# Linear attention on one core: K, V and Q in 4 KB runs over four heads, groups in order, one PSUM pool, the copy of the transposed Q shared by two engines, halved last store

## The chip, the cores and the metric

One core of one Trainium2 chip runs the kernel. The metric is the device time of an execution in microseconds, as a median of several runs; lower is better. A ratio is the mean time of one kernel's fast runs over the mean time of the fast runs of the kernel before in the same rounds, so it is not quite the ratio of the medians quoted beside it. "Span" is the time from the first to the last instruction in one profiled execution; the device time is one to two microseconds longer.

In lines of the profile PE is TensorE, PEld its weight loads, DVE VectorE, ACT ScalarE, POOL GpSimd and SP SyncE. PSUM is the memory that TensorE writes its results to; here it is handed out in eight banks. A row tile is a part of TensorE's rows that one matmul uses. The granted clock is the share of full speed that TensorE was given; "low clock" means 0.5.

## The reference

```python
Q, K, V: float32 (8, 12, 512, 64), normal
Q_feat = np.maximum(0, Q) + 1
K_feat = np.maximum(0, K) + 1
KV = np.einsum('bhkd,bhkv->bhdv', K_feat, V)
K_sum = np.sum(K_feat, axis=2)
numerator = np.einsum('bhqd,bhdv->bhqv', Q_feat, KV)
denominator = np.einsum('bhqd,bhd->bhq', Q_feat, K_sum)
return (numerator / (denominator[:, :, :, None] + 1e-10)).astype(np.float32)
```

## The kernel before

The 96 heads are worked in 12 groups of eight heads. A group loads 1 MiB each of K, V and Q from HBM (cast to bf16 on the way) and stores 1 MiB. Its stages: VectorE makes the features of K and Q; ScalarE copies V into a layout with a column of ones; TensorE accumulates K-features by V (with the sums in the extra column), transposes Q's features, and multiplies the two; VectorE divides. The schedule is a software pipeline: features of one group, first matmul of the group before, output of the one before that.

```python
k_dram = view(K, C)        # C = 8: runs of 8 x 64 x 4 B = 2 KB; Q has view(Q, 2 * C)
...
psum_qt = tile_pool(name="psum_qt", bufs=2)    # 1 bank each
psum_kva = tile_pool(name="psum_kva", bufs=1)  # 2 banks
psum_out = tile_pool(name="psum_out", bufs=2)  # 2 banks each
...
def kv_and_transpose(g):                        # first matmul: two row tiles of 64
    ...
    for half in range(2):
        qt_ps = psum_qt.tile([P, C, P], BF16)   # one PSUM tile for each half
        for c in range(C):
            nc.tensor.transpose(qt_ps[:, c, :], qf[:, half * C + c, :, :], identity)
        nc.scalar.copy(out=qt[:, :, :, half], in_=qt_ps)
...
for it in range(NG + 2):
    if it < NG: features(it)
    if 1 <= it < NG + 1: kv_and_transpose(it - 1)
    if it >= 2: output(it - 2)
    if it + IN_BUFS < NG: load(it + IN_BUFS)
    if it - LAG >= 0: store(it - LAG)
```

Of the kernel before, what the change touches and what calls it, by code (L numbers as in the profile page):

```python
# [8 lines left out]
FP32 = mybir.dt.float32  # L9
BF16 = mybir.dt.bfloat16  # L10
ALU = mybir.AluOpType

BANK = 512
VP = 130
IN_BUFS = 4
OUT_BUFS = 6
LAG = 3


@with_exitstack  # L20
def kernel(
    ctx: ExitStack,
    tc: tile.TileContext,
    Q: bass.AP,
    K: bass.AP,
    V: bass.AP,
    out: bass.AP,
):






    nc = tc.nc

    B, H, S, D = Q.shape
    P = 128
    C = 8
    C2 = 2 * C  # L40
    NPAIR = B * H * S // (P * C)
    NP = 4
    NG = NPAIR // NP
    D1 = D + 1
    W = 2 * D + 1

    def view(t, c):
        return t.flatten_outer_dims().rearrange("(n p c) d -> p n c d", p=P, c=c)

    q_dram = view(Q, C2)  # L50
    k_dram = view(K, C)
    v_dram = view(V, C)
    o_dram = view(out, C)

    const = ctx.enter_context(tc.tile_pool(name="const", bufs=1))
    head_pool = ctx.enter_context(tc.tile_pool(name="head_pool", bufs=1))
    in_pool = ctx.enter_context(tc.tile_pool(name="in_pool", bufs=IN_BUFS))
    feat_pool = ctx.enter_context(tc.tile_pool(name="feat", bufs=2))
    mid_pool = ctx.enter_context(tc.tile_pool(name="mid", bufs=3))
    out_pool = ctx.enter_context(tc.tile_pool(name="out_pool", bufs=OUT_BUFS))  # L60
    recip_pool = ctx.enter_context(tc.tile_pool(name="recip", bufs=4))
    psum_qt = ctx.enter_context(tc.tile_pool(name="psum_qt", bufs=2, space=bass.MemoryType.PSUM))
    psum_kva = ctx.enter_context(tc.tile_pool(name="psum_kva", bufs=1, space=bass.MemoryType.PSUM))
    psum_out = ctx.enter_context(tc.tile_pool(name="psum_out", bufs=2, space=bass.MemoryType.PSUM))

    identity = const.tile([P, P], BF16, name="identity")
    NV = 2
    v_aug = [const.tile([P, 2, C, VP], BF16, name=f"v_aug{i}") for i in range(NV)]

    raw = {}  # L70
    feat = {}
    mid = {}
    outs = {}

    def load(g):
        first = g == 0
        k_raw = (head_pool if first else in_pool).tile(
            [P, NP, C, D], FP32 if first else BF16, name="k_raw"
        )
        v_raw = in_pool.tile([P, NP, C, D], BF16, name="v_raw")  # L80
        q_raw = in_pool.tile([P, 2, C2, D], BF16, name="q_raw")
        (nc.sync if first else nc.gpsimd).dma_start(  # L82
            out=k_raw, in_=k_dram[:, g * NP : g * NP + NP]
        )
        nc.gpsimd.dma_start(out=v_raw, in_=v_dram[:, g * NP : g * NP + NP])  # L85
        nc.gpsimd.dma_start(out=q_raw, in_=q_dram[:, g * 2 : g * 2 + 2])  # L86
        raw[g] = (k_raw, v_raw, q_raw)

    def store(g):
        nc.gpsimd.dma_start(out=o_dram[:, g * NP : g * NP + NP], in_=outs.pop(g))  # L90

    def feature(dst, src):
        nc.vector.tensor_scalar(  # L93
            out=dst, in0=src, scalar1=1.0, scalar2=1.0, op0=ALU.add, op1=ALU.max
        )

    def features(g):
        k_raw, v_raw, q_raw = raw.pop(g)
        kf = feat_pool.tile([P, 2, C, 2, D], BF16, name="kf")
        qf = feat_pool.tile([P, C2, 2, D], BF16, name="qf")  # L100
        va = v_aug[g % NV]
        for h in range(2):
            feature(kf[:, h].rearrange("p c n d -> p n c d"), k_raw[:, h:NP:2])
            nc.scalar.copy(  # L104
                out=va[:, h].rearrange("p c (n x) -> p n c x", n=2)[:, :, :, 0:D],
                in_=v_raw[:, h:NP:2],
            )
        feature(qf.rearrange("p c n d -> p n c d"), q_raw)
        feat[g] = (kf, qf)

    def kv_and_transpose(g):
        kf, qf = feat.pop(g)
        va = v_aug[g % NV]
        kva_ps = psum_kva.tile([P, 2, BANK], FP32, name="kva_ps")
        for h in range(2):
            for c in range(C):
                for j in range(2):
                    nc.tensor.matmul(  # L118
                        kva_ps[:, j, h * W : h * W + W],
                        lhsT=kf[64 * j : 64 * j + 64, h, c, :, :],  # L120
                        rhs=va[64 * j : 64 * j + 64, h, c, 0:W],
                        start=(c == 0),
                        stop=(c == C - 1),
                    )
        kva = mid_pool.tile([P, 2, 2, D1 + 1], BF16, name="kva")
        for n in range(2):
            nc.scalar.copy(  # L127
                out=kva[64 * n : 64 * n + 64, :, :, 0:D1],
                in_=kva_ps[64 * n : 64 * n + 64, :, 0 : 2 * W].rearrange(
                    "p j (h x) -> p j h x", h=2  # L130
                )[:, :, :, D * n : D * n + D1],
            )

        qt = mid_pool.tile([P, C, P, 2], BF16, name="qt")
        for half in range(2):
            qt_ps = psum_qt.tile([P, C, P], BF16, name="qt_ps")
            for c in range(C):
                nc.tensor.transpose(qt_ps[:, c, :], qf[:, half * C + c, :, :], identity)  # L138
            nc.scalar.copy(out=qt[:, :, :, half], in_=qt_ps)  # L139
        mid[g] = (kva, qt)  # L140

    def output(g):
        kva, qt = mid.pop(g)
        o_sb = out_pool.tile([P, NP, C, D], FP32, name="o_sb")
        for h in range(2):
            ops = [psum_out.tile([P, 2, BANK], FP32, tag="o_ps", name="o_ps") for _ in range(2)]
            for c in range(C):
                off = (c % 4) * D1
                for n in range(2):
                    for j in range(2):  # L150
                        b = 2 * h + j
                        nc.tensor.matmul(  # L152
                            ops[n][64 * j : 64 * j + 64, c // 4, off : off + D1],
                            lhsT=qt[64 * n : 64 * n + 64, c, 32 * b : 32 * b + 32, :],
                            rhs=kva[64 * n : 64 * n + 64, j, h, 0:D1],
                            start=True,
                            stop=True,
                        )
            for n in range(2):
                cells = ops[n][:, :, 0 : 4 * D1].rearrange("p b (r x) -> p b r x", x=D1)  # L160
                den = cells[:, :, :, 0:1] if n else cells[:, :, :, D:D1]
                num = cells[:, :, :, 1:D1] if n else cells[:, :, :, 0:D]
                recip = recip_pool.tile([P, 2, 4, 1], FP32, name="recip")
                nc.vector.reciprocal(out=recip, in_=den)  # L164
                nc.vector.tensor_tensor(  # L165
                    out=o_sb[:, 2 * n + h].rearrange("p (b r) d -> p b r d", b=2),
                    in0=num,
                    in1=recip.to_broadcast([P, 2, 4, D]),
                    op=ALU.mult,
                )  # L170
        outs[g] = o_sb

    with tc.manual_schedule():
        for g in range(IN_BUFS):
            load(g)
            if g == 0:
                make_identity(nc, identity)
                for t in v_aug:
                    nc.gpsimd.memset(t[:, :, :, D : D + 1], 1.0)  # L179
        for it in range(NG + 2):  # L180
            if it < NG:
                features(it)
            if 1 <= it < NG + 1:
                kv_and_transpose(it - 1)
            if it >= 2:
                output(it - 2)
            if it + IN_BUFS < NG:
                load(it + IN_BUFS)
            s = it - LAG
            if s >= 0:  # L190
                store(s)
        for s in range(NG + 2 - LAG, NG):
            store(s)


# [28 lines left out]
```

## Time and profile before

| | before |
|---|---|
| device time, median | 131.0 us (130.81 to 132.17, three runs; 131.12 with the fourth) |
| span of the profiled run | 129.8 us |
| moved to and from HBM | 37.75 MB read, 12.58 MB written |
| busy: PE, DVE, ACT | 46%, 44%, 48% of the span |

Read this profile from the transfers: compute engines are half idle, and the chain of work that ended last, followed back from the end, is 72% transfers. The lines that carry this are in the prediction. In a group's line the figures are busy time, mean ns of one, and the idle time of the engine just before them.

```profile
DMA 72%; issue 19%; POOL 4%; POOLq 1%
...
L139 ACT COPY qt<-qt_ps 128x1024 bf16<-128x1024 bf16 x24 | 29.5, 1298 | 0.4
```

Both halves of qt are copied by ScalarE, 1.3 us each, and ScalarE hardly waits for them.

### The profile page before, as it was taken

To read this page: it belongs to the slowest core of one execution; us is meant where nothing else is said; L and a number is where in the kernel's file an instruction comes from. 1 tells how busy PE (TensorE), PEld (TensorE's weight loads), DVE (VectorE), ACT (ScalarE), POOL (GpSimd) and SP (SyncE) were. 2 spreads that over 40 slices of the span, in tenths; PEclk is the share of its full clock that TensorE was granted. 3 is DMA by queue.
4 is the path that set the end of the run, shared out by engine and by line. 5 is a ranking of instruction groups with operands and counts; after the bars stand their busy time and mean duration, and the time that the engine had idled before them with its cause. 6 is when DMAs were issued, how large, how long until landed. Compare 5 with 4: busy or idle time off the path is not lost.

```text
span 129.8 us, 3048 instructions
## 1 busy us (share of the span) xinstructions
PE 59.0 (46%) x1344; PEld 50.5 (39%) x1344; DVE 57.7 (44%) x132; ACT 62.6 (48%) x73; POOL 36.1 (28%) x55
## 2 busy tenths in 40 slices
PE   0008309208758292864939119409606802933200
PEld 0007209107647191753828009308505701922100
DVE  0222212057374775727577077066227407567700
ACT  3023086590966939296690590391095096270000
POOL 6972224222332242224224222422231200202020
PEclk9999965555686959555595865875785685595555
DMA  2999999999999999999999999999999999999853
GB/s 93 321 204 195 210 194 204 210 206 211 205 209 208 209 207 206 210 207 207 277 302 207 253 331 205 231 350 191 218 347 223 212 357 418 420 417 360 341 218 121
DMA packets 19213, 32.17 MB, mean 248 GB/s; under 512 B 768, under 2 KB 12544, under 8 KB 19200
## 3 DMA queue, kind: packets, MB, share of 16 engines
q0 software_dynamic: 18672, 30.94, 106.3%
q1 hardware_dynamic: 528, 1.05, 2.1%
q8 instruction: 10, 0.16, 0.5%
q14 instruction: 3, 0.02, 0.0%
HBM read 37.75 MB, written 12.58 MB: 388 GB/s over the span
## 4 chain that ended last, share of the span: by engine, by line
DMA 72%; issue 19%; POOL 4%; POOLq 1%
DMA out_dram<-o_sb 31%; DMA k_raw<-in_K_dram 16%; DMA q_raw<-in_Q_dram 15%; DMA v_raw<-in_V_dram 9%; POOL out_dram L90 2%; POOLq L219 1%; POOL q_raw L86 1%; POOL k_raw L82 0%; POOL v_raw L85 0%; POOL identity masks.py:199 0%; POOL identity masks.py:197 0%; POOL v_aug L179 0%; POOLq L90 0%; POOLq L86 0%; POOLq L208 0%
## 5 line engine op out<-in xcount | busy, mean ns | idle before, releaser
L104 ACT COPY v_aug<-v_raw 128x1024 bf16<-128x1024 bf16 x24 | 24.1, 1056 | 48.6 <-DMA v_raw<-in_V_dram 48.6
L152 PE MATMUL o_ps<-kva,qt 64*64 64x65 bf16 x768 | 17.3, 229 | 46.9 <-DVE o_sb L165 45.8
L165 DVE TENSOR_TENSOR o_sb<-o_ps,recip 128x512 f32<-128x512 f32 x48 | 33.2, 691 | 1.6
L152 PEld LDWEIGHTS <-qt 64*64 64x64 bf16 x768 | 12.7, 137 | 52.0 <-DVE o_sb L165 48.9
L139 ACT COPY qt<-qt_ps 128x1024 bf16<-128x1024 bf16 x24 | 29.5, 1298 | 0.4
L118 PE MATMUL kva_ps<-v_aug,kf 64*128 64x129 bf16 x384 | 22.3, 302 | 15.4 <-ACT v_aug L104 10.1
L93 DVE TENSOR_SCALAR qf<-q_raw 128x2048 bf16<-128x2048 bf16 x12 | 8.3, 694 | 42.2 <-DMA q_raw<-in_Q_dram 42.2
L118 PEld LDWEIGHTS <-kf 64*128 64x128 bf16 x384 | 19.1, 137 | 16.2 <-issue 15.6
L138 PE MATMUL qt_ps<-identity,qf 128*128 128x128 bf16 x192 | 21.7, 303 | 0.1
L90 POOL DMA_DIRECT2D out_dram<-o_sb x12 | 9.3, 774 | 38.2 <-DVE o_sb L165 19.6
L138 PEld LDWEIGHTS <-qf 128*128 128x128 bf16 x192 | 18.8, 142 | 2.6 <-issue 2.2
L93 DVE TENSOR_SCALAR kf<-k_raw 128x1024 bf16<-128x1024 bf16 (+1 forms) x24 | 9.8, 450 | 11.2 <-DMA k_raw<-in_K_dram 11.1
L164 DVE RECIPROCAL recip<-o_ps 128x8 f32<-128x8 f32 x48 | 9.6, 201 | 10.5 <-PE o_ps L152 10.5
L85 POOL DMA_DIRECT2D v_raw<-in_V_dram x12 | 9.1, 759 | 17.0 <-ACT kva L127 5.4
L82 POOL DMA_DIRECT2D k_raw<-in_K_dram x11 | 8.6, 786 | 16.7 <-DVE kf L93 6.6
L86 POOL DMA_DIRECT2D q_raw<-in_Q_dram x12 | 8.4, 702 | 15.9 <-DMA k_raw<-in_K_dram 9.0
L127 ACT CAST kva<-kva_ps 64x260 bf16<-64x260 f32 x24 | 8.8, 367 | 3.5 <-PE kva_ps L118 3.4
L104 ACT ACT_TABLE_LOAD x1 | 1.3, 1283 | 0.7 <-PEq L208 0.7
masks.py:199 POOL TENSOR_SCALAR_AFFINE_SELECT identity<-identity 128x128 bf16<-128x128 bf16 x1 | 0.3, 287 | 0.1
masks.py:197 POOL MEMSET identity<- 128x128 bf16 x1 | 0.2, 244 | 0.0
L179 POOL MEMSET v_aug<- 128x16 bf16 x2 | 0.2, 175 | 0.0
L208 POOL MEMSET const-float32-0.0<- 128x1 f32 x1 | 0.1, 99 | 0.2 <-issue 0.2
(3 smaller groups left out, 0.3 us busy)
## 6 DMA issues: line engine op xcount, KB each, us to landing
out_dram<-o_sb POOLq DMA_DIRECT2D x12, 1024.0 KB, 20.0
v_raw<-in_V_dram POOLq DMA_DIRECT2D x12, 512.0 KB, 19.7
q_raw<-in_Q_dram POOLq DMA_DIRECT2D x12, 512.0 KB, 19.8
k_raw<-in_K_dram POOLq DMA_DIRECT2D x11, 512.0 KB, 19.7
k_raw<-in_K_dram SPq DMA_DIRECT2D x1, 1024.0 KB, 5.0
```

The lines of the kernel that those rows point to most:

```text
L85: nc.gpsimd.dma_start(out=v_raw, in_=v_dram[:, g * NP : g * NP + NP])
L86: nc.gpsimd.dma_start(out=q_raw, in_=q_dram[:, g * 2 : g * 2 + 2])
L90: nc.gpsimd.dma_start(out=o_dram[:, g * NP : g * NP + NP], in_=outs.pop(g))
L93: nc.vector.tensor_scalar(out=dst, in0=src, scalar1=1.0, scalar2=1.0, op0=ALU.add, op1=ALU.max)
L104: nc.scalar.copy(out=va[:, h].rearrange("p c (n x) -> p n c x", n=2)[:, :, :, 0:D], in_=v_raw[:, h:NP:2],)
L118: nc.tensor.matmul(kva_ps[:, j, h * W : h * W + W], lhsT=kf[64 * j : 64 * j + 64, h, c, :, :], rhs=va[64 * j : 64 * j + 64, h, c, 0:W], st ...
L127: nc.scalar.copy(out=kva[64 * n : 64 * n + 64, :, :, 0:D1], in_=kva_ps[64 * n : 64 * n + 64, :, 0 : 2 * W].rearrange("p j (h x) -> p j h x ...
L138: nc.tensor.transpose(qt_ps[:, c, :], qf[:, half * C + c, :, :], identity)
L139: nc.scalar.copy(out=qt[:, :, :, half], in_=qt_ps)
L152: nc.tensor.matmul(ops[n][64 * j : 64 * j + 64, c // 4, off : off + D1], lhsT=qt[64 * n : 64 * n + 64, c, 32 * b : 32 * b + 32, :], rhs=kv ...
L164: nc.vector.reciprocal(out=recip, in_=den)
L165: nc.vector.tensor_tensor(out=o_sb[:, 2 * n + h].rearrange("p (b r) d -> p b r d", b=2), in0=num, in1=recip.to_broadcast([P, 2, 4, D]), op ...
```

## The change

Its intent: longer runs in HBM for K and V, so that transfers run faster; half of the qt copy moved to VectorE; a simple schedule in which each group is computed and stored before the next; a last store in two halves, so that the end is shorter. With 16 rows of a head per partition, four heads share the 128 partitions, so the first matmul works in four row tiles of 32. There are five output buffers instead of six, and three groups are loaded ahead instead of four. The diff is shortened:

```diff
-    k_dram = view(K, C)
-    v_dram = view(V, C)
+    k_dram = view(K, C2)
+    v_dram = view(V, C2)
...
-    psum_qt / psum_kva / psum_out   (2 x 1, 1 x 2, 2 x 2 banks)
+    psum = tile_pool(name="psum", bufs=4)   # 2 banks each
...
     def store(g):
+        # last group only:
+        for h in range(2):
+            nc.sync.dma_start(out=o_to[:, h:NP:2], in_=o_sb[:, h:NP:2])
...
-                for j in range(2):        # two row tiles of 64, 32 matmuls
+                for b in range(4):        # four row tiles of 32, 64 matmuls
...
         qt = mid_pool.tile([P, C, P, 2], BF16, name="qt")
+        qt_ps = psum.tile([P, 2, C, P], BF16, tag="ps", name="qt_ps")
         for half in range(2):
-            qt_ps = psum_qt.tile([P, C, P], BF16, name="qt_ps")
...
-            nc.scalar.copy(out=qt[:, :, :, half], in_=qt_ps)
+        nc.scalar.copy(out=qt[:, :, :, 0], in_=qt_ps[:, 0])
+        nc.vector.tensor_copy(out=qt[:, :, :, 1], in_=qt_ps[:, 1])
...
-        for it in range(NG + 2):  # features(it), kv(it - 1), output(it - 2), load, store(it - 3)
+        for g in range(NG):
+            if g + AHEAD < NG:
+                load(g + AHEAD)
+            compute(g)
+            store(g)
```

More of the change, by code (lines that the diff above doesn't have):

```diff
@@ L15 @@
 IN_BUFS = 4
-OUT_BUFS = 6
-LAG = 3
+OUT_BUFS = 5
+AHEAD = 3
 @with_exitstack
@@ L61 @@
     recip_pool = ctx.enter_context(tc.tile_pool(name="recip", bufs=4))
-    psum_qt = ctx.enter_context(tc.tile_pool(name="psum_qt", bufs=2, space=bass.MemoryType.PSUM))
-    psum_kva = ctx.enter_context(tc.tile_pool(name="psum_kva", bufs=1, space=bass.MemoryType.PSUM))
-    psum_out = ctx.enter_context(tc.tile_pool(name="psum_out", bufs=2, space=bass.MemoryType.PSUM))
+    psum = ctx.enter_context(tc.tile_pool(name="psum", bufs=4, space=bass.MemoryType.PSUM))
     identity = const.tile([P, P], BF16, name="identity")
     NV = 2
-    v_aug = [const.tile([P, 2, C, VP], BF16, name=f"v_aug{i}") for i in range(NV)]
+    v_aug = [const.tile([P, C2, VP], BF16, name=f"v_aug{i}") for i in range(NV)]
     raw = {}
-    feat = {}
-    mid = {}
     outs = {}
@@ L77, in load @@
         k_raw = (head_pool if first else in_pool).tile(
-            [P, NP, C, D], FP32 if first else BF16, name="k_raw"
+            [P, 2, C2, D], FP32 if first else BF16, name="k_raw"
         )
-        v_raw = in_pool.tile([P, NP, C, D], BF16, name="v_raw")
+        v_raw = in_pool.tile([P, 2, C2, D], BF16, name="v_raw")
         q_raw = in_pool.tile([P, 2, C2, D], BF16, name="q_raw")
         (nc.sync if first else nc.gpsimd).dma_start(
-            out=k_raw, in_=k_dram[:, g * NP : g * NP + NP]
+            out=k_raw, in_=k_dram[:, g * 2 : g * 2 + 2]
         )
-        nc.gpsimd.dma_start(out=v_raw, in_=v_dram[:, g * NP : g * NP + NP])
+        nc.gpsimd.dma_start(out=v_raw, in_=v_dram[:, g * 2 : g * 2 + 2])
         nc.gpsimd.dma_start(out=q_raw, in_=q_dram[:, g * 2 : g * 2 + 2])
@@ L89, in store @@
     def store(g):
-        nc.gpsimd.dma_start(out=o_dram[:, g * NP : g * NP + NP], in_=outs.pop(g))
+        o_sb = outs.pop(g)
+        o_to = o_dram[:, g * NP : g * NP + NP]
+        if g < NG - 1:
+            nc.gpsimd.dma_start(out=o_to, in_=o_sb)
+            return
+        for h in range(2):
+            nc.sync.dma_start(out=o_to[:, h:NP:2], in_=o_sb[:, h:NP:2])
     def feature(dst, src):
@@ L95, in feature, with compute @@
         )
-    def features(g):
+    def compute(g):
         k_raw, v_raw, q_raw = raw.pop(g)
-        kf = feat_pool.tile([P, 2, C, 2, D], BF16, name="kf")
+        kf = feat_pool.tile([P, C2, 2, D], BF16, name="kf")
         qf = feat_pool.tile([P, C2, 2, D], BF16, name="qf")
         va = v_aug[g % NV]
-        for h in range(2):
-            feature(kf[:, h].rearrange("p c n d -> p n c d"), k_raw[:, h:NP:2])
+        kva_ps = [psum.tile([P, 2, BANK], FP32, tag="ps", name="kva_ps") for _ in range(2)]
+        for half in range(2):
+            cs = slice(half * C, half * C + C)
+            feature(kf[:, cs].rearrange("p c n d -> p n c d"), k_raw[:, :, cs])
             nc.scalar.copy(
-                out=va[:, h].rearrange("p c (n x) -> p n c x", n=2)[:, :, :, 0:D],
-                in_=v_raw[:, h:NP:2],
-            )
-        feature(qf.rearrange("p c n d -> p n c d"), q_raw)
-        feat[g] = (kf, qf)
-    def kv_and_transpose(g):
-        kf, qf = feat.pop(g)
-        va = v_aug[g % NV]
-        kva_ps = psum_kva.tile([P, 2, BANK], FP32, name="kva_ps")
-        for h in range(2):
-            for c in range(C):
-                for j in range(2):
+                out=va[:, cs].rearrange("p c (n x) -> p n c x", n=2)[:, :, :, 0:D],
+                in_=v_raw[:, :, cs],
+            )
+            for c in range(half * C, half * C + C):
+                for b in range(4):
+                    ps = slice(32 * b, 32 * b + 32)
                     nc.tensor.matmul(
-                        kva_ps[:, j, h * W : h * W + W],
-                        lhsT=kf[64 * j : 64 * j + 64, h, c, :, :],
-                        rhs=va[64 * j : 64 * j + 64, h, c, 0:W],
+                        kva_ps[b // 2][:, b % 2, 0:W],
+                        lhsT=kf[ps, c, :, :],
+                        rhs=va[ps, c, 0:W],
                         start=(c == 0),
-                        stop=(c == C - 1),
+                        stop=(c == C2 - 1),
                     )
@@ L126, in kv_and_transpose @@
         for n in range(2):
-            nc.scalar.copy(
-                out=kva[64 * n : 64 * n + 64, :, :, 0:D1],
-                in_=kva_ps[64 * n : 64 * n + 64, :, 0 : 2 * W].rearrange(
-                    "p j (h x) -> p j h x", h=2
-                )[:, :, :, D * n : D * n + D1],
-            )
+            ps = slice(64 * n, 64 * n + 64)
+            for h in range(2):
+                nc.scalar.copy(
+                    out=kva[ps, h, :, 0:D1], in_=kva_ps[h][ps, :, D * n : D * n + D1]
+                )
         qt = mid_pool.tile([P, C, P, 2], BF16, name="qt")
+        qt_ps = psum.tile([P, 2, C, P], BF16, tag="ps", name="qt_ps")
         for half in range(2):
-            qt_ps = psum_qt.tile([P, C, P], BF16, name="qt_ps")
+            cs = slice(half * C, half * C + C)
+            feature(qf[:, cs].rearrange("p c n d -> p n c d"), q_raw[:, :, cs])
             for c in range(C):
-                nc.tensor.transpose(qt_ps[:, c, :], qf[:, half * C + c, :, :], identity)
-            nc.scalar.copy(out=qt[:, :, :, half], in_=qt_ps)
-        mid[g] = (kva, qt)
-    def output(g):
-        kva, qt = mid.pop(g)
+                nc.tensor.transpose(qt_ps[:, half, c, :], qf[:, half * C + c, :, :], identity)
+        nc.scalar.copy(out=qt[:, :, :, 0], in_=qt_ps[:, 0])
+        nc.vector.tensor_copy(out=qt[:, :, :, 1], in_=qt_ps[:, 1])
         o_sb = out_pool.tile([P, NP, C, D], FP32, name="o_sb")
         for h in range(2):
-            ops = [psum_out.tile([P, 2, BANK], FP32, tag="o_ps", name="o_ps") for _ in range(2)]
+            ops = [psum.tile([P, 2, BANK], FP32, tag="ps", name="o_ps") for _ in range(2)]
             for c in range(C):
@@ L154, in output @@
                             lhsT=qt[64 * n : 64 * n + 64, c, 32 * b : 32 * b + 32, :],
-                            rhs=kva[64 * n : 64 * n + 64, j, h, 0:D1],
+                            rhs=kva[64 * n : 64 * n + 64, h, j, 0:D1],
                             start=True,
@@ L173 @@
     with tc.manual_schedule():
-        for g in range(IN_BUFS):
+        for g in range(AHEAD):
             load(g)
@@ L178 @@
                 for t in v_aug:
-                    nc.gpsimd.memset(t[:, :, :, D : D + 1], 1.0)
-        for it in range(NG + 2):
-            if it < NG:
-                features(it)
-            if 1 <= it < NG + 1:
-                kv_and_transpose(it - 1)
-            if it >= 2:
-                output(it - 2)
-            if it + IN_BUFS < NG:
-                load(it + IN_BUFS)
-            s = it - LAG
-            if s >= 0:
-                store(s)
-        for s in range(NG + 2 - LAG, NG):
-            store(s)
+                    nc.gpsimd.memset(t[:, :, D : D + 1], 1.0)
+        for g in range(NG):
[3 more added lines that the diff above has]
+            store(g)
 _INS = ['Q', 'K', 'V']
```

## The prediction

> **What bounds the kernel now.** I first read the slices of the page: which row is full, and when.
>
> ```profile
> PE   0008309208758292864939119409606802933200
> DVE  0222212057374775727577077066227407567700
> ACT  3023086590966939296690590391095096270000
> DMA  2999999999999999999999999999999999999853
> GB/s 93 321 204 195 210 194 204 210 206 211 205 209 208 209 207 206 210 207 207 277 302 207 253 331 205 231 350 191 218 347 223 212 357 418 420 417 360 341 218 121
> HBM read 37.75 MB, written 12.58 MB: 388 GB/s over the span
> ```
>
> DMA is at 9 from the second slice to the third from last; no compute row is. GB/s counts a cast load at its bf16 size, so 205 of loading is about 410 read from HBM, like the 418 of the stores at the end: the bound is one rate all through. The chain of waits agrees (72% DMA). Only three things can shorten it: a better rate, a shorter head, less idle in the tail. So next the rate, from the engine views in order of time, by when arrivals release engines:
>
> ```profile
> 34.95 0.69 DVE L93 TENSOR_SCALAR qf<-q_raw 128x2048 bf16<-128x2048 bf16 x1 [1.99 <-DMA q_raw<-in_Q_dram]
> 40.05 2.01 ACT L104 COPY v_aug<-v_raw 128x1024 bf16<-128x1024 bf16 x2 [2.35 <-DMA v_raw<-in_V_dram]
> 42.54 0.69 DVE L93 TENSOR_SCALAR qf<-q_raw 128x2048 bf16<-128x2048 bf16 x1 [2.25 <-DMA q_raw<-in_Q_dram]
> 47.61 2.01 ACT L104 COPY v_aug<-v_raw 128x1024 bf16<-128x1024 bf16 x2 [2.44 <-DMA v_raw<-in_V_dram]
> 50.05 0.69 DVE L93 TENSOR_SCALAR qf<-q_raw 128x2048 bf16<-128x2048 bf16 x1 [1.99 <-DMA q_raw<-in_Q_dram]
> ```
>
> From V to Q, one Q transfer (4 KB runs): 2.49 and 2.44 us; over the nine undisturbed groups the mean is 2.44 us. From Q to the next V, a K and a V transfer (2 KB runs): 5.10 and 5.07; the mean of the six groups before stores mix in is 5.13, or 2.57 each. All three move 1 MiB from HBM, so 2 KB runs cost 0.13 us a transfer more. A store group takes 10.1 us where a load group takes 7.55, so a store is 2.55 us.
>
> Last the tail, in the table of stretches:
>
> ```profile
> core 0: us, PE busy (x) PEld busy (x) DVE busy (x) ACT busy (x) POOL busy (x), PEclk, DMA share, GB/s
> 110.00:115.00 5.00, 4.12 (x110) 3.63 (x110) 2.50 (x6) 2.36 (x4) 0.75 (x1) 0.69 1.03 419
> 115.00:120.00 5.00, 1.63 (x66) 1.17 (x66) 3.62 (x10) 0.84 (x1) 0.75 (x1) 0.65 0.94 380
> 120.00:125.00 5.00, 0.85 (x32) 0.57 (x32) 2.39 (x5) 0.00 (x0) 0.75 (x1) 0.50 0.63 249
> 125.00:131.00 6.00, 0.00 (x0) 0.00 (x0) 0.00 (x0) 0.00 (x0) 0.00 (x0) 0.50 0.42 161
> ...
> out_dram<-o_sb POOLq DMA_DIRECT2D x12, 1024.0 KB, 20.0
> ```
>
> Idle DMA: 0.06 x 5 + 0.37 x 5 + (6 - 0.42 x 6 less the 1.2 us past the end) = 0.3 + 1.9 + 2.3 = 4.5 us. The last store is issued at 123.49 with an empty queue, 1.8 us after the data of its second half could have been ready, and needs 4.7 us to land.
>
> **What the Trainium skill says.** "DMA: Bandwidth & Descriptors", section "Why small descriptors are slow (HBM only)": each packet has a fixed cost on the engine's internal bus and each operation carries its descriptors. The trace agrees in kind: 256 more runs per transfer, 16 per engine, cost 0.13 us, about 8 ns a run. The same page, section "Issuing engines are not separate DMA queues": who issues does not matter for bandwidth, so the store from SyncE buys no rate. "TensorE: Matmul & The Clock Gate", section "Part 3: Packing small matmuls — row/col tiling": tiles in different row groups run together. The trace agrees for two: 32 matmuls of 129 columns took 1.92 us at the low clock, 60 ns each, while a full-height transpose of 128 columns took 1.89/16 = 118 ns. For four row groups no row shows it yet, but in the output stage four loads and four 64x64 matmuls took 0.65/8 = 81 ns together, so weight loads do not queue up either. "VectorE: DVE Perf Modes", errata section, puts a copy from PSUM at 120 cycles plus one per element (0.96 GHz): 1.19 us for 1024, an estimate for the new VectorE copy; the f32 product of 512 elements from PSUM, 0.69 us here, fits that formula (0.66).
>
> **The change part by part.**
>
> Runs. K and V go from 2 KB to 4 KB: 23 GpSimd transfers x 0.13 = 3.0 us less DMA work (perhaps another 0.1 on K of group 0). All of it is on the path, because DMA is full. K, V and Q have one form, so four heads of 32 partitions lie in a tile; that forces the four row tiles and doubles the first matmul from 384 to 768.
>
> Order of transfers. Each group's store follows its own compute; before, eight stores were left behind the last load. Queue now: load g+3 before compute g, then store g, load g+4, and so on. When a group ends, three groups of loads (over 21 us) wait in the queue, so DMA does not starve, though GpSimd now waits for each result. Behind the last load there remain stores 8 to 11.
>
> Compute in order. Per group, one after another from the last product of the group before (low clock, durations from the groups table and starts from the timelines):
> - K features, first half: 0.42; hand-over 0.06.
> - First matmul: 64 in four row tiles, 16 rounds as before: 1.8 to start the transposes (at 2.3).
> - Transposes, 16: 1.9 (4.2). Beside them ScalarE copies kva, now four pieces of 64x130; two of 64x260 took 0.75, I estimate 1.0 for four (3.5), and one qt half, 1.3 (4.8). The Q features (0.76) hide.
> - Second qt half on VectorE: 1.2 (5.5). Before, ScalarE did both, 2.45.
> - Output matmuls of h 0: 0.65 (6.2); those of h 1 hide under VectorE.
> - Reciprocal and product, four pairs at 0.84: 3.35 (9.5).
>
> So a period of 9.5 us at the low clock and about 8.4 at the full one (matmuls 0.5, transposes 0.45, output 0.2 shorter); at the mean clock of 0.67 before, about one third full speed, 9.15. The V copies (2.0) fall into ScalarE's gaps. The DMA period is 3 x 2.44 + 2.55 = 9.87 us. Compute fits beneath, by only 0.7. PSUM: seven buffers a group over four slots; each reuse falls on a buffer emptied in an earlier step of the chain above, so I count no further wait.
>
> Store halves. The first half of group 11 goes out two pairs (1.7 us) before the end; the second moves only 0.5 MiB, 1.3 us, after it.
>
> Sum. DMA of before: span 129.8 less 4.5 tail idle less about 2.3 head = 123.0 us of work. After: 120.0. Last load: 2.3 + 36 x 2.44 + 8 x 2.55 + 1.5 of the irregularities (the before kernel shows gaps of 8.4 to 8.5 us in place of 7.55, some 3 us in all, some of them before this point) = 112.0; notice of it some 1.8 us later, 113.8. Group 11 then needs from Q: features 0.5, transposes 1.9, VectorE copy 1.2, output 0.7, pairs 3.4 = 7.7, so 121.5. Stores 8 to 10 keep DMA busy until 119.7; the first half is issued then and fills to 121.3. The second half: 0.4 issue + 1.3 + about 2 to land = 3.7: the span ends at 125.2. Time over span was 131.0 against 129.8, 1.2 more: 126.4. I add 0.4 for the chance of compute that lags a little: 126.8 us, 3.2% less.
>
> **The rivals.**
> 1. Compute becomes the bound. Group 0 ends at about 19.2 (V at 8.8, Q at 11.2, then the chain). Each 0.1 us of period beyond 9.3 moves the end by 1.0 us: 9.5 (low clock all through) gives a span of 127, time 128.4; 10.0 gives 132, time 133.5. For it: the chain has six hand-overs, and the old software pipeline that hid it is gone; PE sits idle some 3 us per group, which keeps the clock low. Against: PE, ACT and DVE were each under half busy, and the copy shared with VectorE takes 1.2 off the chain.
> 2. The four row tiles do not overlap and 64 matmuls cost 3.4 to 3.8 in place of 1.9. Then the period is over 11 and the time about 145. Two row groups overlap in the trace and the weight loads of four tiles too; I give it 4%.
> 3. The runs do not pay: the 2.44 of Q comes from its place in the queue or from engine hand-over. Whatever hand-over adds to V-to-Q it takes from Q-to-V; but if so the gain is only the tail, 1.5 us: time 129.3. Against: the difference is there in every undisturbed group.
> 4. The rate is hidden: HBM saturates for four groups' mix of loads and stores at 410 to 420 whatever the run. Q's 1.049 MB in 2.44 us is 430 GB/s; that is already above it.
>
> **Range and chances.** Best case, DMA never idle: 2.3 + 120.0 + 2.2 = 124.5, time 125.7; with fewer irregularities 124.8. The upper end is compute at 9.7. 8 in 10: 124.8 to 130.8. Faster by over 2% means below 128.4: it needs a period up to 9.5 and the runs to pay; I give 0.70. Within 2%: 0.24. Slower: 0.06, nearly all compute.
>
> **What would show it.** Right: DMA at 9 to the last two slices; arrivals of V to Q and Q to V in one step of 2.44; VectorE waiting for Q in most groups; the product-to-product period of a group about 9.9 in the middle; the first matmul about 1.9 us for 64; the new VectorE copy near 1.2. Wrong: GpSimd or DMA waiting for o_sb with DMA slices below 9, VectorE without waits for DMA, and a period above 9.9 (rival 1); first-matmul groups of over 3 us (rival 2); K and V still at 2.57 (rival 3).

## The result, and the profile after

| | before | after |
|---|---|---|
| device time, median | 131.12 us | 144.0 us (143.88 to 144.15) |
| ratio | 1 | 1.0957 (1.09 to 1.1014) |
| span | 129.8 us | 142.3 us |
| granted TensorE clock, mean | 0.69 | 0.70 |

The change made the kernel 9.6% slower. Two slices of the page and the shares of the chain, in the kernel after:

```profile
DMA  3999999999999999999999999999999956106125
GB/s 125 296 211 212 211 212 211 211 192 326 223 212 354 215 235 333 211 264 305 211 298 272 211 325 245 212 345 223 225 339 218 248 223 253 58 0 259 40 98 196
...
DVE 42%; PE 36%; ACT 12%; DMA 5%; issue 2%; POOLq 0%
```

The transfers are no longer full to the end: in the last eight slices they are at 6 tenths or less, and in one they move nothing. Before that they are full although compute is late: loads are issued up to three groups ahead of it, so the lag shows only when the last load has landed. Slices of 9 alone do not prove that transfers bind. The chain that ended last is now compute, one engine handing to the next; transfers have 5% of it where they had 72%. Who waited for whom says the same (engine, line, and what it waited for; us in total, times, longest):

```profile
POOL out_dram L89 <- DVE o_sb L161: 81.3, 11, 9.8
ACT kva L126 <- PE kva_ps L115: 64.8, 12, 6.0
DVE qt L138 <- ACT qt L137: 45.4, 12, 4.0
```

GpSimd, which issues loads and stores, spends 81.3 us waiting for results. The third line is the surprise: VectorE's copy of one half of qt waits, in all 12 groups, for ScalarE's copy of the *other* half. Nothing in the data asks for that. One whole group in order of time, at the low clock (start, duration, engine):

```profile
62.65 0.75 DVE L95 TENSOR_SCALAR kf<-k_raw 128x1024 bf16<-128x1024 bf16 x2
...
63.12 1.92 PE L115 MATMUL kva_ps<-v_aug,kf 32*128 32x129 bf16 x64 [3.44 <-DVE kf L95]
...
64.97 1.89 PE L136 MATMUL qt_ps<-identity,qf 128*128 128x128 bf16 x16
65.07 0.87 ACT L126 CAST kva<-kva_ps 64x130 bf16<-64x130 f32 x4 [5.89 <-PE kva_ps L115]
...
66.90 1.29 ACT L137 COPY qt<-qt_ps 128x1024 bf16<-128x1024 bf16 x1 [0.95 <-PE qt_ps L136]
...
68.22 1.29 DVE L138 COPY qt<-qt_ps 128x1024 bf16<-128x1024 bf16 x1 [3.96 <-ACT qt L137]
...
69.57 1.09 PE L148 MATMUL o_ps<-kva,qt 64*64 64x65 bf16 x64 [2.71 <-DVE qt L138]
70.26 0.21 DVE L160 RECIPROCAL recip<-o_ps 128x8 f32<-128x8 f32 x1 [0.75 <-PE o_ps L148]
...
73.63 0.75 DVE L95 TENSOR_SCALAR kf<-k_raw 128x1024 bf16<-128x1024 bf16 x2
```

From one K-feature step to the next: 73.63 - 62.65 = 10.98 us, against the 9.5 of the prediction. Laid beside its chain, counted from 62.65:

| step | predicted | measured |
|---|---|---|
| transposes start | 2.3 | 2.32 |
| ScalarE's copy starts | 3.5 | 4.25 |
| transposes done | 4.2 | 4.21 |
| VectorE's copy starts | 4.3 | 5.57 |
| both halves of qt ready (output matmuls start) | 5.5 | 6.92 |
| first reciprocal | 6.2 | 7.61 |
| next group | 9.5 | 10.98 |

Nearly all of the excess arises in one step, the two copies. The prediction had ScalarE's copy run beside the transposes of the second half, and VectorE's right behind these. Here ScalarE's starts only when both halves are transposed, and VectorE's 1.32 us after that. Over the kernel the first matmul starts at 20.17 in group 1 and at 127.99 in group 11, so the mean period is 10.78 us (in some groups the clock is higher).

### The profile page after: what moved, and what is told of

Read it like the earlier page. It is cut to its first block, busy times and chain, and to the rows that moved or that the text cites. A ratio compares the mean times of both kernels' runs of the same rounds, so it can differ in the third digit from the quotient of the medians.

```text
span 142.3 us, 3858 instructions
## 1 busy us (share of the span) xinstructions
PE 55.6 (39%) x1728; PEld 48.8 (34%) x1728; DVE 74.4 (52%) x156; ACT 49.8 (35%) x85; POOL 36.4 (26%) x54
## 4 chain that ended last, share of the span: by engine, by line
DVE 42%; PE 36%; ACT 12%; DMA 5%; issue 2%; POOLq 0%
DVE o_sb L161 23%; PE kva_ps L115 16%; PE qt_ps L136 15%; DVE qt L138 11%; ACT qt L137 11%; PE o_ps L148 5%; DVE recip L160 5%; DMA v_raw<-in_V_dram 5%; DVE kf L95 3%; ACT v_aug L108 1%; POOLq L195 0%
## 5 line engine op out<-in xcount | busy, mean ns | idle before, releaser
L115 PE MATMUL kva_ps<-v_aug,kf 32*128 32x129 bf16 x768 | 23.0, 308 | 47.4 <-DVE kf L95 38.2
L138 DVE COPY qt<-qt_ps 128x1024 bf16<-128x1024 bf16 x12 | 15.6, 1296 | 45.4 <-ACT qt L137 45.4
L115 PEld LDWEIGHTS <-kf 32*128 32x128 bf16 x768 | 19.9, 140 | 48.8 <-DVE kf L95 39.7
L126 ACT CAST kva<-kva_ps 64x130 bf16<-64x130 f32 x48 | 10.3, 264 | 65.0 <-PE kva_ps L115 64.8
L89 POOL DMA_DIRECT2D out_dram<-o_sb x11 | 10.6, 961 | 81.3 <-DVE o_sb L161 81.3
L148 PE MATMUL o_ps<-kva,qt 64*64 64x65 bf16 x768 | 11.7, 226 | 32.5 <-DVE qt L138 32.5
L148 PEld LDWEIGHTS <-qt 64*64 64x64 bf16 x768 | 10.1, 137 | 35.4 <-DVE qt L138 35.4
L137 ACT COPY qt<-qt_ps 128x1024 bf16<-128x1024 bf16 x12 | 15.5, 1292 | 10.4 <-PE qt_ps L136 10.4
L95 DVE TENSOR_SCALAR qf<-q_raw 128x1024 bf16<-128x1024 bf16 x24 | 11.3, 514 | 3.6 <-DMA q_raw<-in_Q_dram 3.6
L78 POOL DMA_DIRECT2D k_raw<-in_K_dram x11 | 7.9, 714 | 0.5 <-DMA v_raw<-in_V_dram 0.5
```

The costliest lines, as they stand in the source:

```text
L89: nc.gpsimd.dma_start(out=o_to, in_=o_sb)
L95: nc.vector.tensor_scalar(out=dst, in0=src, scalar1=1.0, scalar2=1.0, op0=ALU.add, op1=ALU.max)
L115: nc.tensor.matmul(kva_ps[b // 2][:, b % 2, 0:W], lhsT=kf[ps, c, :, :], rhs=va[ps, c, 0:W], start=(c == 0), stop=(c == C2 - 1),)
L126: nc.scalar.copy(out=kva[ps, h, :, 0:D1], in_=kva_ps[h][ps, :, D * n : D * n + D1])
L137: nc.scalar.copy(out=qt[:, :, :, 0], in_=qt_ps[:, 0])
L138: nc.vector.tensor_copy(out=qt[:, :, :, 1], in_=qt_ps[:, 1])
```

## The experiments

Every kernel below gives the correct result unless it says otherwise.

**Copies into separate stretches of qt.** The first suspicion was qt: the two copies write interleaved elements of one tile. So each copy takes four of the eight columns c, for both halves, and reads a PSUM bank of its own.

```diff
-        qt_ps = psum.tile([P, 2, C, P], BF16, tag="ps")
+        qt_ps = psum.tile([P, 2, 2, C // 2, P], BF16, tag="ps")
-  transpose(qt_ps[:, half, c, :], ...)
+  transpose(qt_ps[:, c // 4, half, c % 4, :], ...)
-        nc.scalar.copy(out=qt[:, :, :, 0], in_=qt_ps[:, 0])
-        nc.vector.tensor_copy(out=qt[:, :, :, 1], in_=qt_ps[:, 1])
+        for u, copy in enumerate((nc.scalar.copy, nc.vector.tensor_copy)):
+            copy(out=qt[:, 4*u : 4*u+4].rearrange("p c q t -> p t c q"), in_=qt_ps[:, u])
```

> Theory A (the two qt copies run one after the other because they write interleaved elements of one tile, 1.3 us more per group than I had counted): with the copies split by c, so that each writes its own stretch of qt and reads its own PSUM bank, VectorE's copy starts together with ScalarE's, the period of a group falls from 10.8 to about 9.5 us, and the span from 142.3 to about 128, time 129.5 to 130.5. Theory B (what costs is that VectorE, the engine of the chain, has been given more work): the period stays above 10.5 and the time within 1% of 144.0.

It took 141.55 us, ratio 1.0735 (1.0679 to 1.0791), outside the times of both theories: the form of theory A that blamed qt fell. The trace shows why:

```profile
86.43 1.29 ACT L138 COPY qt<-qt_ps 128x1024 bf16<-128x1024 bf16 x1 [0.95 <-PE qt_ps L136]
...
87.76 1.30 DVE L138 COPY qt<-qt_ps 128x1024 bf16<-128x1024 bf16 x1 [3.96 <-ACT qt L138]
87.78 0.44 PE L151 MATMUL o_ps<-kva,qt 64*64 64x65 bf16 x16 [1.38 <-ACT qt L138]
```

TensorE treats the two stretches of qt as separate: 16 output matmuls start right after ScalarE's copy. VectorE still waits for it. With this early start the period at the low clock is 10.78 us (93.43 - 82.65 between first matmuls) in place of 10.98, which makes 2.2 of the 2.5 us gained; the order of the copies has another cause.

**Both copies on ScalarE.**

```diff
-        nc.vector.tensor_copy(out=qt[:, :, :, 1], in_=qt_ps[:, 1])
+        nc.scalar.copy(out=qt[:, :, :, 1], in_=qt_ps[:, 1])
```

> Both qt copies on ScalarE again, the rest of the change kept. Theory A (the copies are serial on whatever engine): the chain keeps two copies in a row, some 0.1 us shorter for back-to-back starts on one engine, time 142.5 to 144.5. Theory B (VectorE's added load): VectorE loses 1.3 us per group and the time falls to 128 to 131.

139.19 us, ratio 1.0526 (1.0437 to 1.0614); one of the four runs is slow, and the median of the three fast ones is 138.66. This is outside both expectations, but nearer to A: relieving VectorE of 1.3 us in each of 12 groups brought back 5.3 us, not 13. The copies remain serial, and back to back on one engine they start 1.16 us apart instead of 1.32 (78.30 - 77.14 in its trace, which is of the slow run; the interval is taken, not a time). Eleven groups of 0.16 make 1.8 of the 5.3 us. The rest I did not separate; the mean granted clock does not order the fast runs (137.94 us at 0.697, 139.72 at 0.751). So the second copy on VectorE not only failed to help, it cost a hand-over.

**The transfers alone, in 4 KB and in 2 KB runs.** Both give a wrong result: all loads and stores of the changed kernel in its order, no compute, stores of zeros. The second has K and V as in the kernel before.

```diff
     def compute(g):
-        ...
+        raw.pop(g)
+        outs[g] = zeros[g % 2]
```

> Wrong result on purpose: the transfers of the changed kernel in its order, without any compute (stores send zeros). It gives the floor that the transfers alone set. My prediction's sum says 124.5 of span less what compute waits cost, so a time of 123.5 to 126. If the runs of 4 KB do not pay, 127 to 129.

> The same with K and V in runs of 2 KB as before; wrong result on purpose. If 2 KB runs cost 0.13 us a transfer: 24 x 0.13 = 3.1 us more than the 4 KB form. If the gap between arrivals that I read was a matter of hand-over (rival 3 of the prediction): under 1 us more.

130.18 us (129.84 to 130.73) and 130.78 us (130.47 to 131.11), ratios 0.9878 and 0.9928, with intervals that overlap. The first run missed both of its ranges. The second took 0.6 us more than the first, not 3.1: that is what its other expectation, the one for rival 3, had (under 1 us). Each issue on GpSimd waits here for an earlier transfer to land, so the steps between issues are those between landings. In 4 KB runs:

```profile
73.07 0.70 POOL L78 DMA_DIRECT2D k_raw<-in_K_dram  x1 [1.68 <-DMA k_raw<-in_K_dram]
75.55 0.71 POOL L81 DMA_DIRECT2D v_raw<-in_V_dram  x1 [1.78 <-DMA v_raw<-in_V_dram]
78.00 0.71 POOL L82 DMA_DIRECT2D q_raw<-in_Q_dram  x1 [1.74 <-DMA q_raw<-in_Q_dram]
80.56 0.78 POOL L89 DMA_DIRECT2D out_dram<-zeros  x1 [1.85 <-DMA out_dram<-zeros]
83.02 0.70 POOL L78 DMA_DIRECT2D k_raw<-in_K_dram  x1 [1.69 <-DMA k_raw<-in_K_dram]
```

and in 2 KB runs:

```profile
64.07 0.74 POOL L78 DMA_DIRECT2D k_raw<-in_K_dram  x1 [1.74 <-DMA k_raw<-in_K_dram]
66.59 0.74 POOL L81 DMA_DIRECT2D v_raw<-in_V_dram  x1 [1.78 <-DMA v_raw<-in_V_dram]
69.04 0.70 POOL L82 DMA_DIRECT2D q_raw<-in_Q_dram  x1 [1.71 <-DMA q_raw<-in_Q_dram]
71.61 0.79 POOL L89 DMA_DIRECT2D out_dram<-zeros  x1 [1.87 <-DMA out_dram<-zeros]
74.13 0.74 POOL L78 DMA_DIRECT2D k_raw<-in_K_dram  x1 [1.73 <-DMA k_raw<-in_K_dram]
```

The step to a V is 2.48 against 2.52 us, to a Q 2.45 in both, to a store 2.56 and 2.57, to a K 2.46 against 2.52. Longer runs save 0.04 to 0.06 us per transfer, 0.11 per group (9.95 against 10.06), 1.3 us over 12 groups at most; the times differ by 0.6. The 0.13 that the prediction read was two to three times that. Beside compute the saving is of the same size or a little larger. Where a store stands in each group, V reaches ScalarE 10.11 us after the V of the group before in the kernel before, and 9.94 us after it in a later run with K and V in 4 KB runs ("Both apart"); the first two lines are from the one, the last two from the other:

```profile
62.81 2.01 ACT L104 COPY v_aug<-v_raw 128x1024 bf16<-128x1024 bf16 x2 [2.46 <-DMA v_raw<-in_V_dram]
72.92 2.01 ACT L104 COPY v_aug<-v_raw 128x1024 bf16<-128x1024 bf16 x2 [4.97 <-DMA v_raw<-in_V_dram]
...
72.76 2.01 ACT L109 COPY v_aug<-v_raw 128x1024 bf16<-128x1024 bf16 x2 [2.33 <-DMA v_raw<-in_V_dram]
82.70 2.01 ACT L109 COPY v_aug<-v_raw 128x1024 bf16<-128x1024 bf16 x2 [2.81 <-DMA v_raw<-in_V_dram]
```

Most groups of the second kind are 9.94 to 9.95 apart, those of the kernel before 10.07 to 10.15 (10.05 to 10.06 with only its last store halved): 0.1 to 0.2 us a group, 0.05 to 0.1 for each of K and V.

The times of the two kernels without compute must not be taken as a floor. In the 4 KB form data stop at about 124.5 us, and 3.8 us pass before the span ends; with 2 KB it is about 126 and 2.7. The kernel after needs 1.3 us from its last data to its end. I did not find out what these idle kernels do in between.

**The halves of the transposed Q in two PSUM tiles.** What is still shared by the two copies in the first experiment is the PSUM tile they read. So each half gets its own tile; as all eight banks are taken, the common pool has three slots instead of four. The copies write interleaved elements of qt as in the change.

```diff
-    psum = tile_pool(name="psum", bufs=4)
+    psum = tile_pool(name="psum", bufs=3)        # 2 banks each
+    psum_qt = tile_pool(name="psum_qt", bufs=2)  # 1 bank each
-        qt_ps = psum.tile([P, 2, C, P], BF16, tag="ps")
+        qt_ps = [psum_qt.tile([P, C, P], BF16) for _ in range(2)]
```

> The two halves of the transposed Q in two PSUM tiles of their own (pool of three for the rest), the copies into interleaved elements of qt as in the change. If it is the shared PSUM tile that orders the two copies (theory A1): they start together, or ScalarE's even before the second half's transposes are done; period about 9.5 us, time 129.5 to 132. If it is the interleaved writes into qt (theory A2): VectorE's copy still starts at the end of ScalarE's, period above 10, time 138 to 144; ScalarE's may start up to 0.9 us earlier.

131.52 us, ratio 0.9994 (0.9939 to 1.0048; one of four runs is slow, the fast ones have a median of 131.35): theory A1, as expected.

```profile
77.27 0.75 DVE L96 TENSOR_SCALAR kf<-k_raw 128x1024 bf16<-128x1024 bf16 x2
...
79.59 1.89 PE L137 MATMUL qt_ps<-identity,qf 128*128 128x128 bf16 x16
79.69 0.87 ACT L127 CAST kva<-kva_ps 64x130 bf16<-64x130 f32 x4 [5.23 <-PE kva_ps L116]
80.66 1.29 ACT L138 COPY qt<-qt_ps 128x1024 bf16<-128x1024 bf16 x1
81.58 1.29 DVE L139 COPY qt<-qt_ps 128x1024 bf16<-128x1024 bf16 x1 [2.62 <-PE qt_ps L137]
...
83.02 0.70 PE L149 MATMUL o_ps<-kva,qt 64*64 64x65 bf16 x34 [1.54 <-DVE qt L139]
```

ScalarE's copy starts while the second half is still being transposed, and VectorE's waits for its transposes alone; they overlap although they write interleaved elements. Counted from the K features, ScalarE's copy starts at 3.39 and the output matmuls at 5.75, where the prediction had 3.5 and 5.5 and the change 4.25 and 6.92. The period is 9.81 us in these groups (107.32 - 97.51 between two first matmuls). This one edit takes away the whole loss of 12.5 us against the kernel before. That both engines read PSUM side by side at 1.29 us each agrees with the Trainium skill, "PSUM — Partial Sum Buffer", section "Specifications (TRN2)", which says that ScalarE and VectorE can access it in parallel without loss unless they hit the same bank. The halves lay in different banks in the change too (8 x 128 x 2 B = 2 KB each); it is the one tile that kept them in order.

**Is it the tile or the pool?** That run changed both the pool and the tile. This one, made last, changes the pool only.

```diff
+    psum_qt = tile_pool(name="psum_qt", bufs=1)  # 2 banks
-        qt_ps = psum.tile([P, 2, C, P], BF16, tag="ps")
+        qt_ps = psum_qt.tile([P, 2, C, P], BF16)
```

> The pools of the psum-apart run (three for the rest, one of its own for the transposed Q), but the transposed Q stays one tile of two banks, as in the change. If the one tile orders the two copies: VectorE's copy starts at the end of ScalarE's again, period above 10.3, 139 to 145. If it was the shared pool (slots and their release) that held VectorE's copy: they overlap, 131 to 132.5.

144.04 us, ratio 1.0947 (1.0899 to 1.0996), the time of the change itself, with the order back:

```profile
88.70 1.29 ACT L138 COPY qt<-qt_ps 128x1024 bf16<-128x1024 bf16 x1 [0.95 <-PE qt_ps L137]
90.02 1.29 DVE L139 COPY qt<-qt_ps 128x1024 bf16<-128x1024 bf16 x1 [3.96 <-ACT qt L138]
```

It is the tile. The shared pool was innocent, as the prediction had counted it. What in the tile does it was not looked at: it may be that waits are put in for a tile as a whole when the program is built; no run shows that.

**Both apart.** Two PSUM tiles, and the copies split by c as in the first experiment.

> Both apart: two PSUM tiles and the copies into two separate stretches of qt (split by c). If either of the two sharings orders the copies, neither is left: the copies start together, period about 9.3 to 9.6, time 129.5 to 132. If the copies are still serial, neither theory holds.

129.22 us, ratio 0.982 (0.9767 to 0.9872), slightly better than expected. ScalarE's copy starts at 78.60 and VectorE's at 78.89, and the period in a group where VectorE does not wait for data is 9.15 us (84.44 - 75.29 between first matmuls). Now transfers bind again: the chain that ended last is

```profile
DMA 85%; DVE 4%; PE 3%; issue 3%; ACT 1%; POOL 0%; POOLq 0%; DVEq 0%; ACTq 0%
```

**K features one group ahead.** This leaves the serial copies as they are and shortens the chain elsewhere: VectorE makes the K features of the next group before the products of this one, so the next first matmul runs beside them.

```diff
+        if g + 1 < NG:
+            k_features(g + 1)
         o_sb = out_pool.tile(...)
         ...  # output matmuls, reciprocals, products
```

> The change with only the K features of the next group put ahead of the output of this one on VectorE; the two copies stay serial. Theory C (the in-order chain of a group on VectorE is the bound): the first matmul and part of the transposes slip under the products, the period falls to about 8.6 us if transfers allow, so transfers bind again: 130 to 132.5. If the serial copies alone were the trouble: above 138.

130.93 us, ratio 0.9963 (0.9918 to 1.0007), as theory C has it. Early, while data is there in time, the first matmuls start 9.1 us apart (17.40, 26.46, 35.59, 44.71; I had expected 8.6); in 11 of the 12 groups ScalarE's copy of V waits for its data (33.0 us in all), and later the period is that of the transfers. So the serial copies were harmful only because each group's chain ran in order on VectorE; either cure suffices.

**The halved last store alone, in the kernel before.**

```diff
     def store(g):
+        if g < NG - 1: (as before); otherwise:
+        for h in range(2):
+            nc.sync.dma_start(out=o_to[:, h:NP:2], in_=o_sb[:, h:NP:2])
```

> The kernel before with only the halved last store on SyncE. The first half goes out 1.7 us earlier and the second moves half the bytes: 0.5 to 1.5 us less, ratio 0.988 to 0.997. If the end of the kernel is set by a slow rest of the transfers and not by the last store: no change.

129.67 us, ratio 0.9861 (0.9816 to 0.9905): a little more than expected. Alone, this small part of the change is worth 1.7 us, where the version with both apart gains 2.1 in the same rounds; that the gain there has the same source is not shown.

**Towards the best version.** With the copies apart, what is idle is the tail. The table of stretches in that run (the last three columns are the granted clock, the busy share of the 16 DMA engines, and GB/s):

```profile
115.00:120.00 5.00, 3.98 (x98) 3.28 (x88) 2.06 (x3) 2.76 (x6) 0.00 (x0) 0.50 1.02 411
120.00:123.00 3.00, 1.12 (x48) 0.85 (x48) 2.44 (x7) 0.00 (x0) 0.00 (x0) 0.50 0.37 147
123.00:127.60 4.60, 0.00 (x0) 0.00 (x0) 0.88 (x3) 0.00 (x0) 0.00 (x0) 0.50 0.60 228
```

The stores behind the last load run out at 120, and group 11 is ready only at 122 to 124. So four runs: K features ahead on top of the copies apart; each store issued one group later, which puts a fourth store behind the last load; both; and both with the last store in four parts.

```diff
-OUT_BUFS = 5
+OUT_BUFS = 6
             compute(g)
-            store(g)
+            if g >= 1:
+                store(g - 1)
+        store(NG - 1)
```

> Copies apart (as in the last run but two) plus the K features one group ahead. In the copies-apart run the groups already wait for V and Q, and what is left idle is the tail, where group 11 needs 7.9 us after Q arrives. A shorter period cannot shorten that: 128.5 to 129.6, same as copies apart alone. If compute still held transfers back in the middle: under 128.

129.23 us, ratio 0.9831 (0.979 to 0.9871): no gain over copies apart, as expected.

> Copies apart, and each store issued one group later (six output buffers), so that four stores instead of three lie behind the last load in the queue. The hole of about 3 us in the transfers before the last store fills, the last load lands 2.5 us earlier: 126.8 to 128.2, ratio about 0.97. If the period of about 9.3 cannot follow loads that come faster early on: 129 or more.

128.23 us, ratio 0.9767 (0.9725 to 0.9809): the direction is right; the time is just above its range, and the gain over the run with K features ahead, in the same rounds, is 1.0 us. Q of group 11 is there at 112.9 in its trace, against 116.0.

> All three: copies apart, K features ahead, stores one group later. The compute has slack, the tail is covered: 126.5 to 128.0, at or up to 1 us below the run without K features ahead.

128.13 us, ratio 0.9752 (0.9712 to 0.9793), just above the range and not to be told from the run before it. The hole is closed:

```profile
115.00:120.00 5.00, 1.93 (x68) 1.25 (x65) 3.90 (x8) 1.27 (x1) 0.00 (x0) 0.50 1.00 403
120.00:122.00 2.00, 0.00 (x0) 0.00 (x0) 0.71 (x2) 0.00 (x0) 0.00 (x0) 0.50 0.95 380
122.00:124.00 2.00, 0.00 (x0) 0.00 (x0) 0.00 (x0) 0.00 (x0) 0.00 (x0) 0.50 0.73 287
```

> The same with the last store in four parts, each issued when its product is done. The last part moves 0.25 MiB instead of 0.5: 0 to 0.6 us less than the run with halves; more issue work on SyncE may take it back.

128.02 us, ratio 0.9748 (0.9706 to 0.979): not to be told from halves. This is the lowest median, 2.5% below the kernel before, with a span of 126.2 us of which the transfers fill all but the head and the last 3 to 4 us.

## Why the prediction was right or wrong

It forecast 126.8 us, 3.2% less; the kernel took 144.0.

- **What bounds the kernel before: right.** Transfers do; with the compute of the change repaired, the chain is transfers again and no version had a median below 128.0. The period of 9.87 us that it gave the transfers was measured as 9.94 to 9.95 in most groups.
- **The step that failed** is in the chain of a group: "Second qt half on VectorE: 1.2 (5.5). Before, ScalarE did both, 2.45." It took the two copies as parallel, ScalarE's from 3.5 on. They are serial, since both halves lie in one PSUM tile: ScalarE's copy waits for the transposes of both halves (4.25), VectorE's for ScalarE's, and both are ready at 6.92, not 5.5. Put in that 1.4 us and the chain is 10.9 against 10.98 measured. The runs with one tile (144.0, 144.04) and with two (131.52) show that this is the whole loss against the kernel before. It is not the whole error of the forecast: with the overlap that it counted on, the change took 131.52, still above its upper end of 130.8, at a period of 9.81 instead of 9.5.
- **Its consequence was foreseen as rival 1.** "Each 0.1 us of period beyond 9.3 moves the end by 1.0 us": the mean period of 10.78 gives 14.8 us on top of the 125.2 of span, 140.0; the span was 142.3. Eleven periods follow group 0, so the rule should have been 1.1, which gives 141.5. The signs named for it came: GpSimd waiting for o_sb, DMA slices below 9, VectorE almost without waits for data. The margin that the prediction counted on, 0.7 us of period, was half of the term that rested on an untested overlap. I gave a slowdown 6%.
- **The gain of longer runs was mis-sized.** "23 GpSimd transfers x 0.13 = 3.0 us less DMA work": the transfers alone show 0.04 to 0.06 each, 1.3 us at most, and the times of the two forms differ by 0.6; beside compute it was 0.05 to 0.1 each. The 0.13 came from arrivals read on two engines, V's at ScalarE's start and Q's at VectorE's. Q's 2.44 was good (2.45 measured alone); K and V, 2.57, were not (2.52 alone). Hand-over between the two engines is not all of the rest: GpSimd's own issues in the kernel before are 2.59 apart for a V and 2.46 to 2.48 for a Q. Where it came from stays open. Rival 3 was half right: the runs paid, but less than was counted. The halved last store in the kernel before (129.67) came near its value for the tail alone, 129.3.
- **Four row tiles: right.** 64 matmuls of four row tiles take 1.92 us, as 32 of two did. Rival 2 did not occur.
- **PSUM slots and transfer order: right.** No wait of TensorE for a slot shows in the change; the own-pool run changed nothing. What my sum of transfers did not have is the hole of 3 us before the last store: with the copies apart, Q of group 11 came at 116.0 and not at 113.8, so the first half of the last store went out at 122.3 and not at 119.8, when the other stores had run out.
- **VectorE's copy: 1.2 estimated, 1.30 measured**, a small part of the excess.
- **Two readings of the kernel before were off.** The 1.2 us from span to time set the median of other runs against the profiled span; that execution took 131.53, 1.7 more than its span. And that the last store was issued 1.8 us after its second half could have been ready is not borne out as it is worded: it was issued at 123.49, the last product ended at 123.19, the last one of the first half at 120.72.

## What to carry to other kernels

When two engines are to share the emptying of PSUM, give each a PSUM tile of its own, and look in the waits for one copy waiting on the other: two halves of one tile were copied one after the other here even though they lay in different banks and the halves of the destination did not depend on each other. Before replacing a software pipeline by groups in order, add up the chain of one group hand-over by hand-over, and ask of each overlap in the sum what shows it; a margin smaller than one such overlap is none. And when transfers are the bound, take rates from transfers measured alone, and look at the tail first: issuing the last store in two halves, and keeping enough stores behind the last load, gave 1.7 and 1.0 us here, where the transfers alone show 1.3 us at most for the longer runs.

## What the Trainium skill lacked or had wrong

- "TensorEngine Tiling (Array Packing)", section "PSUM Bottleneck", advises to use both ScalarE and VectorE to empty PSUM. It lacks the warning that two engines' copies from one PSUM tile come out in order: 144.04 us with one tile of two banks, 131.52 with two tiles of one bank. "PSUM — Partial Sum Buffer", section "Specifications (TRN2)", makes the bank the condition, by which the two halves, in different banks, would run side by side.
- "DMA: Bandwidth & Descriptors" has no trn2 figure for what the step from 2 KB to 4 KB runs is worth: 2.48 and 2.46 us a MiB of f32 read in 4 KB runs with a cast to bf16, 2.52 in 2 KB.
- "VectorE: DVE Perf Modes", errata section: its 120 cycles plus one per element give 1.19 us for 1024 elements; the copy from PSUM to every second bf16 element took 1.30.
- "TensorE: Matmul & The Clock Gate", Part 3, gives a measured gain for four row tiles over one and none for four over two: 32 matmuls of 64 rows and 64 of 32 rows took the same 1.92 us here.
